# Sixteen partitions of the last load through GpSimd's software queue, in an RMSNorm-Swish kernel

## The chip, the cores and the metric

The kernel runs on one core of one Trainium2 chip. The metric is the device time of one execution in microseconds (us), as the median of several executions. An execution's time is about 1.3 us longer than the span of its profile (161.31 us and 160.0 us).

## The reference

```python
x = randn(16, 1024, 512); gamma = ones(512); eps = 1e-5      # float32
rms = sqrt(mean(x ** 2, axis=-1, keepdims=True) + eps)
x_norm = x / rms * gamma
out = x_norm * sigmoid(x_norm)
```

The kernel reads 33.6 MB and writes 33.6 MB.

## The kernel before

The 16384 rows are cut into eleven tiles. A tile is [128 partitions, sz rows each, 512], so a partition's piece of a tile of 8 rows is 16 KB, contiguous in memory. SyncE issues all loads, ScalarE issues all stores, each on a hardware queue of its own. The tiles lie in a ring of 96 row slots; tile 10, the last one, takes the slots of the second half of tile 3 and so can be loaded once store 3 has landed.

```python
sizes = [4, 4, 8] + [16] * 6 + [8, 8]
ring = 96; cn = 4                         # a chunk is 4 row slots
...
def load(t):
    ...                                   # waits for the stores whose slots it takes
    return nc.sync.dma_start(out=buf(t), in_=dram(xf, t)).then_inc(ld[t], 16)
...
for k in range(K):                        # GpSimd: (mean square + eps) ** -0.5, 32 chunks
    need(nc.gpsimd.tensor_scalar(out=aeps[:, k, :], in0=ms[:, k, :], ...), s_sum, k + 1)...
    need(nc.gpsimd.tensor_tensor(out=rstd[:, k, :], ..., op=ALU.pow), s_eps, k + 1)...
...
def store(t):                             # ScalarE
    need(nc.scalar.dma_start(out=dram(of, t), in_=buf(t)), s_swish, ends[t]).then_inc(st[t], 16)
```

ScalarE squares (3 rows into PSUM, 1 row with its own accumulator), VectorE sums the squares and multiplies by the row's factor and gamma, ScalarE applies Silu in place.

## Time and profile before

| | before |
|---|---|
| time, median of 3 | 160.29 us (160.28 to 160.62) |
| the profiled execution | 161.31 us, span 160.0 us |
| busy | VectorE 87%, ScalarE 78%, GpSimd 41% |
| DMA | 420 GB/s on average, 67.14 MB |

The page of the kernel before: the DMA rows of the slices (40 slices of 4 us; busy tenths, then GB/s), the queues (q1 is SyncE's, q10 ScalarE's; packets, MB, share of the 16 engines' time), and the chain that ended last.

```profile
DMA  6999999989999999999999999999999999999994
GB/s 250 444 487 393 393 381 455 475 358 477 426 408 442 414 483 395 418 483 410 401 461 451 393 442 459 401 451 442 426 393 455 414 442 442 467 401 405 430 434 180
...
q1 hardware_dynamic: 1584, 33.56, 49.3%
q10 hardware_dynamic: 1592, 33.56, 48.8%
q14 instruction: 3, 0.02, 0.0%
...
DVE xb L215 48%; DVE ms L204 29%; DMA xb<-in_x_dram 13%; ACT xb L178 1%; ACT sq L166 1%; ACT junk L159 0%; SPq L118 0%; ACTq L158 0%
```

The chain names VectorE, and VectorE indeed never pauses between 25 and 148.8 us. But the two queues together hold the 16 DMA engines for 98% of the span. To decide between the two, look at the end. This is the timeline of the kernel before (start, duration, engine, line, operation; in brackets the idle time before):

```profile
143.81 0.34 ACTq L183 DMA_DIRECT2D out_dram<-xb  x1
144.33 1.39 POOL L148 TENSOR_TENSOR rstd<-aeps,neg_half 128x4 f32<-128x4 f32 x1
146.18 1.91 ACT L178 ACTIVATE xb<-xb 128x2048 f32<-128x2048 f32 x1 [2.40 <-DVE xb L215]
148.83 1.91 ACT L178 ACTIVATE xb<-xb 128x2048 f32<-128x2048 f32 x1 [0.74 <-DVE xb L215]
150.77 0.34 ACTq L183 DMA_DIRECT2D out_dram<-xb  x1
```

The last two stores (2 MB each) are issued at 143.81 and 150.77 us. In these transfers each of the sixteen DMA engines increments the transfer's semaphore (a counter that other engines wait on) when its share has landed, so the trace has sixteen landings of each:

```
store 9 :  153.06 153.13 153.14 153.25 153.26 153.30 153.37 153.42 153.43 153.44 153.47 153.53 153.71 153.72 153.90 155.11
store 10:  157.91 157.98 157.99 158.09 158.12 158.16 158.21 158.26 158.28 158.29 158.31 158.37 158.55 158.56 158.74 159.96
```

When store 10 is issued, store 9 still needs 2.3 us. Store 10 then lands one transfer time (eight packets of 16 KB that follow each other every 0.607 us, 4.86 us) after store 9. The end is thus bound by the DMA engines; VectorE has some 2 us of slack (an estimate from these 2.3 us). One engine is 1.2 us late.

### The profile page before, as it was taken

The page shows a single profiled execution, that of the slowest core. Times are in us where ns is not written, and L with a number is a line of the kernel's source. Part 1 is how long each engine was busy: PE and PEld are TensorE (multiplying, and loading weights), DVE is VectorE, ACT ScalarE, POOL GpSimd, SP SyncE. Part 2 cuts the span into 40 slices and gives each one's busy share as a digit, 9 for nine tenths or more (in the row PEclk, how much of TensorE's full clock was granted, in tenths as well). Part 3 has the DMA queues.
Part 4 walks back from the last instruction along what each step waited for, and adds up shares of the span by engine and source line. Part 5 has one row for each costly group of instructions (what it writes and reads, how often), then busy time and mean ns, then how long its engine had stood idle before and what let it go on. Part 6 is the DMA issues. An engine that isn't in the chain of part 4 may idle for free.

```text
span 160.0 us, 437 instructions
## 1 busy us (share of the span) xinstructions
DVE 139.1 (87%) x162; ACT 125.1 (78%) x129; POOL 65.5 (41%) x70
## 2 busy tenths in 40 slices
DVE  0298986999999999999999999999999999999100
ACT  1839849888888889988888888888899888884400
POOL 1043552444555555444444445555554444444000
DMA  6999999989999999999999999999999999999994
GB/s 250 444 487 393 393 381 455 475 358 477 426 408 442 414 483 395 418 483 410 401 461 451 393 442 459 401 451 442 426 393 455 414 442 442 467 401 405 430 434 180
DMA packets 3179, 67.14 MB, mean 420 GB/s; under 512 B 356, under 2 KB 356, under 8 KB 360
## 3 DMA queue, kind: packets, MB, share of 16 engines
q1 hardware_dynamic: 1584, 33.56, 49.3%
q10 hardware_dynamic: 1592, 33.56, 48.8%
q14 instruction: 3, 0.02, 0.0%
HBM read 33.56 MB, written 33.55 MB: 419 GB/s over the span
## 4 chain that ended last, share of the span: by engine, by line
DVE 77%; DMA 13%; ACT 2%; issue 0%; SPq 0%; ACTq 0%
DVE xb L215 48%; DVE ms L204 29%; DMA xb<-in_x_dram 13%; ACT xb L178 1%; ACT sq L166 1%; ACT junk L159 0%; SPq L118 0%; ACTq L158 0%
## 5 line engine op out<-in xcount | busy, mean ns | idle before, releaser
L215 DVE SCALAR_TENSOR_TENSOR xb<-xb,rstd,gamma_sb 128x512 f32<-128x512 f32 x128 | 87.4, 747 | 0.0
L178 ACT ACTIVATE xb<-xb 128x2048 f32<-128x2048 f32 x32 | 61.1, 1908 | 16.3 <-DVE xb L215 16.3
L204 DVE TENSOR_REDUCE ms<-sq 128x3 f32<-128x1536 f32 x32 | 56.1, 1754 | 9.7 <-ACT sq L166 9.6
L141 POOL TENSOR_SCALAR aeps<-ms 128x4 f32<-128x4 f32 x32 | 20.7, 646 | 75.9 <-DVE ms L204 75.9
L166 ACT ACTIVATE sq<-xb 128x1536 f32<-128x1536 f32 x32 | 45.9, 1433 | 0.0
L148 POOL TENSOR_TENSOR rstd<-aeps,neg_half 128x4 f32<-128x4 f32 x32 | 44.0, 1376 | 2.7
L159 ACT ACTIVATE junk<-xb 128x512 bf16<-128x512 f32 x32 | 19.7, 615 | 5.7 <-DMA xb<-in_x_dram 5.7
L159 ACT ACTIVATION_READ_ACCUMULATOR junk<-xb 128x1 f32 x32 | 6.0, 187 | 0.0
L190 ACT ACT_TABLE_LOAD x1 | 1.3, 1283 | 3.6 <-issue 3.6
L136 POOL MEMSET gamma<- 128x512 f32 x1 | 0.5, 526 | 1.5 <-POOLq L65 1.5
L228 DVE STREAM_SHUFFLE gamma_sb<-gamma 128x512 f32<-128x512 f32 x1 | 0.7, 720 | 0.0
L255 POOL MEMSET const-float32-0.0<- 128x1 f32 x1 | 0.1, 99 | 0.2 <-issue 0.2
L255 POOL MEMSET const-bfloat16-1.0<- 128x1 bf16 x1 | 0.1, 103 | 0.0
L255 POOL MEMSET const-uint8-127<- 128x1 uint8 x1 | 0.1, 102 | 0.0
L137 POOL MEMSET neg_half<- 128x4 f32 x1 | 0.1, 102 | 0.0
L255 POOL MEMSET const-float32-1.0<- 128x1 f32 x1 | 0.1, 99 | 0.0
L228 DVE LOAD_MASK_SELECT gamma_sb<-gamma x1 | 0.0, 15 | 0.0
## 6 DMA issues: line engine op xcount, KB each, us to landing
xb<-in_x_dram SPq DMA_DIRECT2D x6, 4096.0 KB, 44.5
out_dram<-xb ACTq DMA_DIRECT2D x6, 4096.0 KB, 29.8
xb<-in_x_dram SPq DMA_DIRECT2D x3, 2048.0 KB, 38.5
out_dram<-xb ACTq DMA_DIRECT2D x3, 2048.0 KB, 11.3
xb<-in_x_dram SPq DMA_DIRECT2D x2, 1024.0 KB, 5.9
out_dram<-xb ACTq DMA_DIRECT2D x2, 1024.0 KB, 19.8
gamma<-in_gamma_dram ACTq DMA_DIRECT2D x1, 8.0 KB
```

The costliest lines, as they stand in the source:

```text
L136: nc.gpsimd.memset(gamma4, 0.0).then_inc(s_zero, 1)
L137: nc.gpsimd.memset(neg_half, -0.5).then_inc(s_half, 1)
L141: nc.gpsimd.tensor_scalar(out=aeps[:, k, :], in0=ms[:, k, :], scalar1=eps_f, scalar2=None, op0=ALU.add,),
L148: nc.gpsimd.tensor_tensor(out=rstd[:, k, :], in0=aeps[:, k, :], in1=neg_half, op=ALU.pow),
L159: acc = nc.scalar.activation(out=junk[k % 2], in_=xb[:, at + n_sq, :], func=AF.Square, scale=inv_d**0.5, accum_out=ms[:, k, n_sq : n_sq + 1],)
L166: square = nc.scalar.activation(out=sq[k % 2][:, 0:n_sq, :], in_=xb[:, at : at + n_sq, :], func=AF.Square, scale=inv_d**0.5,)
L178: nc.scalar.activation(out=rows, in_=rows, func=AF.Silu), s_norm, k + 1
L190: nc.scalar.preload_act_table_set("silu_and_others")
L204: nc.vector.tensor_reduce(out=ms[:, k, 0:n_sq], in_=sq[k % 2][:, 0:n_sq, :], op=ALU.add, axis=mybir.AxisListType.X,),
L215: ins = nc.vector.scalar_tensor_tensor(out=row, in0=row, scalar=rstd[:, k, j : j + 1], in1=gamma_sb, op0=ALU.mult, op1=ALU.mult,)
L228: nc.vector.stream_shuffle(gamma_sb, gamma4, [0] * 32), s_gld, 16
L255: nc = _bacc.Bacc("TRN2", target_bir_lowering=False, num_devices=1)
```

## The change

The intent is to even out the DMA engines: engines 0 to 3 are held to be the late ones (the trace does not number the engines). Sixteen of the 128 partitions of the last load, one eighth of it, leave SyncE's queue and go through GpSimd's, first twelve, then four. Tiny transfers of 4 and 8 rows between them are to turn that queue's choice of engines, so that the twelve fall on engines 4 to 15 and the four on 4 to 7. The core of the diff:

```diff
+    blank = [sbuf(f"blank{i}", [8, 16]) for i in range(3)]
...
+    split = 112
     def load(t):
...
+        if t == T - 1:
+            return nc.sync.dma_start(
+                out=buf(t)[0:split], in_=dram(xf, t)[0:split]
+            ).then_inc(ld[t], 16)
         return nc.sync.dma_start(out=buf(t), in_=dram(xf, t)).then_inc(ld[t], 16)
...
+    def turn(count):
+        nc.gpsimd.dma_start(
+            out=blank.pop()[0:count, :], in_=gamma[0 : 16 * count].rearrange("(p n) -> p n", n=16)
+        ).then_inc(s_turn[0], 16)
+        s_turn.pop(0)
+
+    def load_rest(t):
+        ...                               # waits for store 3
+        nc.gpsimd.dma_start(
+            out=buf(t)[split : split + 12], in_=dram(xf, t)[split : split + 12]
+        ).then_inc(s_rest[0], 16)
+        turn(4)
+        nc.gpsimd.dma_start(
+            out=buf(t)[split + 12 : P], in_=dram(xf, t)[split + 12 : P]
+        ).then_inc(s_rest[1], 16)
+        turn(8)
+
+    turn(4)
     for k in range(K):
+        if k == 19:
+            load_rest(T - 1)
...                                       # ScalarE, before the first chunk of tile 10:
+            if t == T - 1:
+                nc.scalar.wait_ge(s_rest[0], 16)
+                nc.scalar.wait_ge(s_rest[1], 16)
```

More of the change, by code (lines that the diff above doesn't have):

```diff
@@ L81 @@
     st = [nc.alloc_semaphore(f"st{t}") for t in range(T)]
+    blank = [sbuf(f"blank{i}", [8, 16]) for i in range(3)]
+    s_turn = [nc.alloc_semaphore(f"s_turn{i}") for i in range(3)]
+    s_turns = list(s_turn)
+    s_rest = [nc.alloc_semaphore(f"s_rest{i}") for i in range(2)]
     s_gld = nc.alloc_semaphore("s_gld")
@@ L138 @@
     nc.gpsimd.wait_ge(s_half, 1)
+    def turn(count):
[4 more added lines that the diff above has]
+    def load_rest(t):
+        _, sz, at = tiles[t]
+        for u in range(t):
+            if tiles[u][2] < at + sz and at < tiles[u][2] + tiles[u][1]:
+                nc.gpsimd.wait_ge(st[u], 16)
+        nc.gpsimd.dma_start(
[7 more added lines that the diff above has]
+    turn(4)
     for k in range(K):
+        if k == 19:
+            load_rest(T - 1)
         need(
@@ L233 @@
             norm(k - 1)
+    for sem in s_turns:
+        nc.sync.wait_ge(sem, 16)
     for t in range(T):
```

## The prediction

> **What bounds the kernel now.** The chain of waits ends on VectorE (77%), and VectorE has no gap from 25 us to 148.8 us. I nevertheless read the end as bound by the DMA engines. The last store (2 MB) is issued at 150.77 us and lands at 159.96 us. The landings of the last four stores (one increment of the semaphore per DMA engine, read from the trace) follow each other by just the time of their packets: 138.5-139.2, 148.2-149.0, 153.1-153.9, 157.9-158.7 us. So at 150.77 the engines still hold 2.3 us or more of the store before; VectorE has that much slack. The page's slices show DMA at 9 tenths or more almost everywhere, 420 GB/s on average.
>
> In each of these stores one engine of the sixteen lands late: 140.57, 150.26, 155.11, and 159.96 against 158.74 for the next. Followed back packet by packet, this engine moved as many bytes as the others but lost some 1.2 us in stalls after 45 us (a 0.3 us gap at 48.0, longer packets near 81, 101, 121 and 127 us). A 16 KB packet takes 0.611 us, so it is two packets late, and it alone sets the end.
>
> **What the change does.** Load 10 (2 MB, landed 133.3 us) shrinks from 8 to 7 packets of 16 KB per engine. Sixteen partitions go through GpSimd: 12 meant for engines 4-15, then 4 meant for engines 4-7[...]. Engines 0-3 then carry one packet less, 8-15 as before, 4-7 one more. [...]
>
> **Worth on the critical path.** If the late engine is one of 0-3 (the gamma load of 4 rows marks four engines, two with the same 0.3 us gap; the late one isn't marked, but my tracing is uncertain in the first 20 us), its end moves by -0.61 us; engines 4-7 move by +0.61, from at most 158.4 to 159.0 (last packets). Best case: about 159.7 us. If it is another engine: 0 to +0.6 us.
>
> **Costs.**
> - GpSimd issues four transfers before chunk 19 (about 89 us; their buffer is free, store 3 landed at 79.6). GpSimd idles some 2.2 us per chunk of 4.3 us. [...]
> - [...]
>
> **Prediction.** 160.0 us, range 159.2 to 161.6. Faster by over 2%: 1%; within 2%: 93%; slower by over 2%: 6%.
>
> **What would show it.** Right: the straggler of the last store lands about 0.6 us after the others, not 1.2; four engines have 99 packets' worth of bytes less one; VectorE's gap near 90 us is under 2.3 us; the last store still queues behind the one before. Wrong: the straggler keeps 1.2 us (not among 0-3, or the sixteen partitions fell on other engines); packets of load 10 longer than 0.611 us [...]; VectorE idle over 2.3 us near chunk 19, with the DMA running dry before the last store.
>
> **What would make it wrong.** [...] stalls of a DMA engine that wander from run to run, so that no fixed choice of engines helps.

The forecast came to 160.0 us, range 159.2 to 161.6: the 160.29 us known of the kernel before, 0.61 us less at best or up to 0.6 us more if the late engine is another, and two costs on top, for the time of GpSimd's issues and for the writes to the sixteen partitions.

## The result and the profile after

The time went from 160.28 us (median of 4, 160.17 to 160.62) to 164.56 us (median of 4, 164.28 to 165.68). The ratio is 1.0276, with a 95% interval of 1.0226 to 1.0326: slower. Ratios here are the mean time of one kernel's fast runs over that of the other's fast runs of the same rounds, so they are not quite the ratio of the medians quoted. The profile after is of an execution of 164.28 us.

The page of the kernel after, the same lines as before. q0 is GpSimd's software queue.

```profile
DMA  6998998998999999999999999999999999999992
GB/s 249 448 462 386 402 485 356 430 501 360 438 404 422 466 436 434 402 491 402 418 475 394 426 298 380 438 406 414 446 458 410 414 446 426 426 450 394 426 438 117
...
q1 hardware_dynamic: 1568, 33.29, 49.2%
q10 hardware_dynamic: 1592, 33.56, 48.1%
q0 software_dynamic: 160, 0.26, 0.6%
q14 instruction: 3, 0.02, 0.0%
...
DVE xb L252 47%; DVE ms L241 29%; DMA xb<-in_x_dram 13%; ACT xb L215 1%; ACT sq L203 1%; ACT junk L196 0%; SPq L128 0%; ACTq L192 0%
```

The chain of waits looks as before and explains nothing: VectorE still never pauses. The difference is in the GB/s row: slices 24 and 25 (94 to 102 us) fell from 442 and 459 to 298 and 380. The engines are still counted as fully busy there (9 tenths): they hold packets, but the packets take longer.

The same in four stretches of the kernel before and then of the kernel after (stretch in us, its length, busy time of VectorE, ScalarE and GpSimd with instruction counts, clock, DMA share, GB/s):

```profile
85.00:92.00 7.00, 7.00 (x9) 6.09 (x7) 2.55 (x4) 1.00 1.00 431
92.00:100.00 8.00, 8.00 (x10) 7.09 (x9) 3.91 (x4) 1.00 1.04 451
100.00:108.00 8.00, 8.00 (x11) 7.09 (x9) 4.09 (x4) 1.00 0.99 426
108.00:116.00 8.00, 8.00 (x11) 7.10 (x9) 4.09 (x4) 1.00 1.01 434
```

```profile
85.00:92.00 7.00, 7.00 (x8) 6.09 (x7) 4.65 (x8) 1.00 1.03 445
92.00:100.00 8.00, 8.00 (x10) 7.09 (x8) 3.73 (x4) 1.00 1.01 337
100.00:108.00 8.00, 8.00 (x11) 7.09 (x9) 4.09 (x4) 1.00 1.00 418
108.00:116.00 8.00, 8.00 (x11) 7.09 (x9) 4.09 (x4) 1.00 1.00 430
```

VectorE and ScalarE are as busy as before in every stretch. From 92 to 100 us the DMA moved 337 in place of 451 GB/s at the same share of busy time.

This is what GpSimd spends on it, from the timeline of the kernel after:

```profile
89.41 0.61 POOL L161 DMA_DIRECT2D xb<-in_x_dram  x1
89.79 1.75 DVE L241 TENSOR_REDUCE ms<-sq 128x3 f32<-128x1536 f32 x1
89.91 1.91 ACT L215 ACTIVATE xb<-xb 128x2048 f32<-128x2048 f32 x1 [0.46 <-DVE xb L252]
90.01 0.52 POOL L151 DMA_DIRECT2D blank<-in_gamma_dram  x1
90.52 0.52 POOL L165 DMA_DIRECT2D xb<-in_x_dram  x1
91.03 0.52 POOL L151 DMA_DIRECT2D blank<-in_gamma_dram  x1
91.46 2.73 DVE L252 SCALAR_TENSOR_TENSOR xb<-xb,rstd,gamma_sb 128x512 f32<-128x512 f32 x4
91.64 0.65 POOL L175 TENSOR_SCALAR aeps<-ms 128x4 f32<-128x4 f32 x1
```

Four issues take 2.1 us and just fit into the idle time that GpSimd has in a chunk (2.2 us). Nobody waits for them. The last store is issued at 150.64 us, no later than before (150.77), and lands 3 us later:

```
store 10 after:  159.62 159.80 159.81 160.04 160.12 160.16 160.33 160.36 160.40 160.44 160.49 160.93 161.37 162.11 162.71 162.93
```

Two things have happened to the landings. All engines are later: the mean of the sixteen went from 158.36 to 160.72 us. And they have drawn apart: four of them stand 0.4 to 2 us behind the twelfth.

The packets show the first of these directly. An undisturbed packet of 16 KB takes 0.611 us and one of 32 KB takes 1.213 us; after 50 us, nine in ten packets of the kernel after keep to that within 3 ns. I call the time above that a packet's excess, and sum it over all packets from 50 us on; beside the sum I count the packets with more than 0.1 us. Before, the excess is 1.7 us, with 4 such packets. After, it is 35.6 us, with 53, and 33.0 us of it falls between 88 and 116 us, while the sixteen partitions are moved: seven of the sixteen packets took 1.0 to 1.3 us instead of 0.611, and 32 KB packets of SyncE's queue at that time took up to 1.99 us longer. 35.6 us over sixteen engines are 2.2 us each.

### The profile page after: what moved, and what is told of

Read it like the earlier page. It is cut to its first block, busy times and chain, and to the rows that moved or that the text cites. A ratio compares the mean times of both kernels' runs of the same rounds, so it can differ in the third digit from the quotient of the medians.

```text
span 163.0 us, 443 instructions
## 1 busy us (share of the span) xinstructions
DVE 139.1 (85%) x162; ACT 125.2 (77%) x129; POOL 68.3 (42%) x75
## 4 chain that ended last, share of the span: by engine, by line
DVE 76%; DMA 13%; ACT 2%; issue 0%; SPq 0%; ACTq 0%
DVE xb L252 47%; DVE ms L241 29%; DMA xb<-in_x_dram 13%; ACT xb L215 1%; ACT sq L203 1%; ACT junk L196 0%; SPq L128 0%; ACTq L192 0%
## 5 line engine op out<-in xcount | busy, mean ns | idle before, releaser
L151 POOL DMA_DIRECT2D blank<-in_gamma_dram x3 | 1.8, 590 | 0.3 <-POOL neg_half L147 0.3
L161 POOL DMA_DIRECT2D xb<-in_x_dram x1 | 0.6, 609 | 0.0
L165 POOL DMA_DIRECT2D xb<-in_x_dram x1 | 0.5, 518 | 0.0
```

The source lines that it names most:

```text
L151: nc.gpsimd.dma_start(out=blank.pop()[0:count, :], in_=gamma[0 : 16 * count].rearrange("(p n) -> p n", n=16)).then_inc(s_turn[0], 16)
L161: nc.gpsimd.dma_start(out=buf(t)[split : split + 12], in_=dram(xf, t)[split : split + 12]).then_inc(s_rest[0], 16)
```

## The experiments

Three theories, and a fourth question:

- **Partitions** (the expectations call it the port theory). Packets that are written at the same time to these sixteen partitions, 112 to 127, hold each other up. The runs can show whether the partitions written make the difference.
- **Software queue.** GpSimd's queue itself, or its extra packets (128 of its 160 are of 4 bytes), slows the engines.
- **Placement.** The packets fell on other engines than intended, and the uneven counts are the loss.
- And: was the late engine of the profile before a property of the kernel at all?

Each experiment was correct against the reference. The first four ran together on one chip, and so did the next four. Kernel before beside them: 160.28 us (160.04 to 160.60). The diffs are shortened; those of the first five runs are against the kernel after.

### The same partitions from a hardware queue

```diff
-        nc.gpsimd.dma_start(out=buf(t)[112:124], ...)     # and [124:128], with three turns
+        nc.scalar.wait_ge(st[3], 16)
+        nc.scalar.dma_start(out=buf(t)[112:124], ...)     # and [124:128], no turns
```

> The same 12 and 4 partitions are loaded from ScalarE's hardware queue at the same chunk; GpSimd issues no transfer and nothing turns. Port theory [...]: the loss stays, 163 to 165 us, with packets lengthened by 0.3 to 2 us while these 16 packets move, in sum 20 to 35 us. Software-queue theory (GpSimd's queue itself costs the DMA engines their time): back to 160 to 161 us, no lengthened packets. Placement alone [...]: 160.9 us, one packet of 0.61 us later than before.

Measured: 163.85 us (163.82 to 165.22), ratio 1.0245 (1.0203 to 1.0288). Excess: 36.0 us, 53 packets over 0.1 us. The slow stretch moved with the transfers, which now stand in line behind ScalarE's stores and landed at 117 to 121 us. The same four stretches of this run:

```profile
85.00:92.00 7.00, 7.00 (x9) 6.09 (x7) 2.55 (x4) 1.00 1.00 431
92.00:100.00 8.00, 8.00 (x10) 7.09 (x8) 3.90 (x4) 1.00 1.04 451
100.00:108.00 8.00, 8.00 (x11) 7.09 (x9) 4.09 (x4) 1.00 0.97 418
108.00:116.00 8.00, 8.00 (x11) 7.09 (x9) 4.67 (x3) 1.00 1.04 346
```

No GpSimd transfer is left, and nearly the whole loss is. On this queue the loads of twelve and of four partitions have twelve and four landings (and one update each at their issue), so twelve engines and four take part. Followed from packet to packet (the way is described under the tiny transfers below), the four are the engines of the gamma load, have one of the twelve packets as well, and land last, the last of them 2.0 us behind the mean.

The last store was issued later in this run, at 152.10 us. ScalarE's two extra issues (85.8 and 86.2 us) are not the reason. From 113.4 us on GpSimd's addition of eps took 2.65 us in place of 0.66, and at the end VectorE waited for GpSimd once (who waited for whom: us in total, times, longest us):

```profile
DVE xb L239 <- POOL rstd L155: 1.2, 1, 1.2
```

Why GpSimd slowed there is not known. The store before the last landed from 153.90 to 157.68 us, so the DMA engines were not idle at 152.10 us and the delay did not set the end.

### The same bytes from GpSimd, as a row of every partition

```diff
-            out=buf(t)[0:112], in_=dram(xf, t)[0:112]                  # SyncE
+            out=buf(t)[:, 0:7, :], in_=dram(xf, t)[:, 0:7, :]
-            out=buf(t)[112:124] ...                                    # GpSimd, two and three turns
+            out=buf(t)[:, 7:8, :], in_=dram(xf, t)[:, 7:8, :]          # GpSimd, one transfer
```

> GpSimd's queue moves the same 256 KB of the last load, but as one row of all 128 partitions instead of sixteen whole partitions[...]. Port theory: 160 to 161 us, few lengthened packets near 93 us. Software-queue theory: 162.5 us or more, as after the change.

Measured: 160.52 us (160.39 to 160.54), ratio 1.0015 (1.0000 to 1.0030). Excess: 1.2 us. The slow stretch of this run, and then its software queue:

```profile
92.00:100.00 8.00, 8.00 (x10) 7.09 (x8) 3.77 (x4) 1.00 0.99 425
```

```profile
q0 software_dynamic: 80, 0.26, 0.4%
```

The same 0.26 MB through the same software queue cost nothing that matters. The software-queue theory falls. (The packets are of another size here, 64 of 4 KB in place of 16 of 16 KB. The pair of runs with sixteen neighbouring and with every eighth partition, below, leaves the size alone.)

### The tiny transfers alone

```diff
-            out=buf(t)[0:112] ...                         # SyncE
+            out=buf(t) ...                                # whole again
-        nc.gpsimd.dma_start(out=buf(t)[112:124] ...)      # and [124:128]
         turn(4)                                           # the three turns stay
         turn(8)
```

> Only the three tiny transfers through GpSimd; the last load is whole again on the hardware queue. Port and placement theories: 160.0 to 160.8 us. Software-queue theory (cost by the transfer, not by the byte): 161.5 us or more. [...]

Measured: 160.28 us (160.17 to 160.40), ratio 1.0002 (0.9986 to 1.0017). They are free. They also did not do what they were for, which was to turn the queue's choice of engines. The trace does not number the engines, so I followed each engine from packet to packet: the next packet of an engine starts within a few ns of the end of the last, and each engine is given eight packets and one semaphore write of every transfer of 128 partitions on the hardware queues, as the counts of the kernel before have it (its eleven loads have sixteen landings each and left 1584 packets, 11 × 16 × 9). Two engines can be taken for one another where they are in step, so this is a reconstruction, not a record. Four engines hold the gamma load of 4 rows. The first turn of 4 rows lies on the same four. The second turn of 4 lies on three of these and a fourth that I take for the other one, swapped on the way; the turn of 8 holds three of them, that one, and four others. Resolved another way, the ties put the second turn on two engines of the gamma load and two others. In both, the turn of 8 holds all four engines of the turn before it, where a queue that moves on would have left them out.

### One transfer of sixteen partitions, no turns

```diff
-        nc.gpsimd.dma_start(out=buf(t)[112:124] ...)      # turn(4), [124:128], turn(8)
+        nc.gpsimd.dma_start(out=buf(t)[112:128], in_=dram(xf, t)[112:128])
-    turn(4)
```

> One GpSimd transfer of all sixteen partitions, no tiny transfers: one packet for each engine, so all engines carry equal bytes again. Port theory: still slow, 162.5 to 165 us, with lengthened packets in sum 20 to 35 us. Placement theory (the engines' uneven counts are the loss): back to 160.0 to 160.6 us. Software-queue theory: between, since there is one transfer in place of five.

Measured: 162.62 us (161.81 to 162.89), ratio 1.0140 (1.0103 to 1.0178). Excess: 35.1 us, as after the change. The software queue left 32 packets, as many as a data packet and a semaphore write for each of sixteen engines. But the landings of the last store lie close together again (the last at 161.09 us, 0.6 us above the mean of 160.46; after the change the last stands 2.2 us above its mean). So the loss has two parts of about the same size: 2.3 us because packets take longer, and 1.9 us more when the sixteen go as twelve and four.

### The change without its turns

```diff
-    turn(4)              # before the loop; and turn(4), turn(8) inside load_rest
```

> The change without its three tiny transfers: GpSimd issues the transfers of 12 and of 4 partitions, nothing between. If the queue hands out engines in a circle, 12 and then 4 fill all sixteen engines evenly, and the time falls to that of one transfer of 16, 162.6 us. If every transfer starts at engine 0 (so the tiny ones turned nothing), the four lowest engines still get two packets each, the time stays at 164.0 to 165.0 us, and four landings of the last store stand 1 to 2.5 us behind the rest.

Measured: 164.30 us (163.22 to 165.02), ratio 1.0257 (1.0199 to 1.0315). The last four landings are 161.34, 161.51, 162.06 and 162.38 us, against a mean of 160.47. Twelve and then four, dealt in a circle, would fill sixteen engines evenly and give the 162.6 us of the run before. They do not: the time stays that of the full change. The reconstruction agrees: four engines have both, eight have one, four have none, and the four with both are the four that land last. In that of the full change, too, four engines have both; they are the last three and the fifth from the end, and at least three of them are engines of the gamma load.

### Sixteen neighbouring partitions against every eighth

These two kernels are the kernel before plus four GpSimd loads of 128 KB into a spare buffer, sixteen partitions of 8 KB each, at chunks 12, 16, 20 and 24. They differ only in the partitions written.

```diff
+            nc.gpsimd.dma_start(out=spare[112:128], in_=dram(xf, T - 1)[112:128, 0:4, :])   # first kernel
+            nc.gpsimd.dma_start(out=spare[0:128:8], in_=dram(xf, T - 1)[112:128, 0:4, :])   # second kernel
```

> The kernel before, with four extra GpSimd loads of 128 KB into a spare buffer, on partitions 112 to 127. The bytes alone cost 4 times 0.3 us, so 161.5 us. Port theory: [...] 163.5 to 165.5 us, with lengthened packets in sum 35 to 60 us.

> As the run before it with the same bytes, packets and queue, but on every eighth partition[...]. Port theory: [...] 161.8 to 163 us, with lengthened packets in sum 10 to 20 us, a third of the other's. If sixteen-partition transfers are slow as such, both are equally slow.

| | time (us) | ratio, 95% | profiled execution | excess | mean landing of the last store |
|---|---|---|---|---|---|
| partitions 112 to 127 | 164.48 (163.92 to 164.61) | 1.0257 (1.0234 to 1.0281) | 164.61 us | 52.6 us, 91 packets over 0.1 us | 162.81 us |
| every eighth partition | 162.95 (162.16 to 163.31) | 1.0162 (1.0128 to 1.0195) | 162.16 us | 7.7 us, 28 packets over 0.1 us | 160.02 us |

The GB/s row of the page of the first and then of the second; both moved 67.67 MB:

```profile
GB/s 265 435 458 433 341 506 363 419 502 387 411 427 421 458 456 413 405 385 474 443 311 474 393 458 251 466 401 421 421 373 445 482 417 425 409 482 393 405 441 301
```

```profile
GB/s 244 450 481 391 391 418 416 471 367 467 471 414 399 424 454 399 456 464 399 432 424 448 424 432 424 397 448 440 401 430 444 436 428 456 424 424 448 391 440 261
```

The first dips to 311 and to 251 where two of its four transfers run (slices 21 and 25), the second nowhere. Source, bytes, packets and queue are the same and the intervals of the ratios do not overlap, so the partitions written make the difference; by what mechanism is not shown.

How large it is, is less certain. In the profiles the second's excess is a seventh of the first's, not the third that I expected. But the first profile is of the slowest of its four executions and the second of the fastest. By the medians the two are 4.20 and 2.67 us over the kernel before; less 1.22 us for the bytes that is 3.0 and 1.5 us, about a half. So every eighth partition may not be free either.

Within each profile the excess accounts for the mean landing. An engine's packets of 8 KB follow each other every 0.306 us, so four times 128 KB are 4 × 0.306 = 1.22 us for each engine. Take the excess over that of the kernel before (1.1 us in its second profile, below) and spread it on 16 engines. Then the first should be late by 1.22 + (52.6 − 1.1) / 16 = 4.4 us and is late by 162.81 − 158.34 = 4.5 us; the second by 1.22 + (7.7 − 1.1) / 16 = 1.6 us and is late by 1.7 us.

### The kernel before, profiled again

> The kernel before once more, for a second profile. If the late engine of the first profile (1.2 us behind in the last store, in an execution that took 161.3 us, 1 us over the median) is a property of the kernel, it is late by 1.2 us again; if it was that execution's, the last landing stands 0.3 to 0.7 us behind the next and the span is 159.0 us.

Measured: one execution of 160.06 us (state unknown), span 158.7 us. Landings of the last store: 157.88 to 158.59 us, and the last at 158.70 us. No engine is late. The queues of that run hold 98.8% of the engines' time:

```profile
q1 hardware_dynamic: 1584, 33.56, 49.7%
q10 hardware_dynamic: 1592, 33.56, 49.1%
```

In this execution, then, the lateness was absent: it belonged to the one that was first profiled, which at 161.31 us was 1 us over the kernel's median. What delayed it there is not known; one packet of 32 KB took 0.56 us longer at 126.9 us, with nothing else to be seen beside it.

## Why the prediction was wrong

The time predicted was 160.0 us (159.2 to 161.6); it was 164.56 us. Point by point:

- **The DMA engines bound the end, not VectorE.** Right. VectorE's work was not touched in the change, and the time follows the landings in every run.
- **The cost of writing to the sixteen partitions.** This is the step that failed. The prediction allowed a small cost for it, for a reason that no trace had shown. Measured: 35.6 us of excess in place of 1.7, which is 2.1 us for each engine, 2.3 us of time in the run with one transfer of sixteen. The longer packets of the sixteen themselves, seven of 1.0 to 1.3 us instead of 0.611, are not all of it. By the reconstruction of the full change even the four engines that carried none of the sixteen lost 1.9 to 2.3 us between 93 and 103.5 us, each mostly in one 32 KB packet of SyncE's queue of 3.0 to 3.1 us. What these four waited for was not tested. The 32 KB packet that took 1.99 us longer came, by the reconstruction, right behind one of the sixteen on its engine; whether it waited because of that was not tested either.
- **"12 meant for engines 4-15, then 4 meant for engines 4-7."** The prediction priced mainly the case that the queue's choice of engines turns. This is the second step that failed: it does not for these transfers. In the trace of the kernel after, each of the five GpSimd transfers, of 4, 8 and 12 partitions, has sixteen landings, where the gamma load of 4 rows on ScalarE's hardware queue has four (and one update at its issue). The five left 160 packets, 32 for each: 16 of 16 KB, 16 of 64 bytes and 128 of 4 bytes. That is as many as a data packet, or a 4-byte one in its place, and a semaphore write for each of sixteen engines in each transfer. So, by the reconstruction, four engines got both packets, three of them at least engines of the gamma load: 7 + 2 against 7 + 1 and 7 + 0. Going as twelve and four cost another 1.9 us. The four packets of the second group took only 0.61 to 0.91 us, so their own lengthening is not the bulk of it. By the reconstruction the engine that lands last has one packet more than the mean (0.61 us) and 3.2 us of excess against a mean of 2.2; together 1.6 of the 1.9 us. Why its packets waited longer than the others' is not shown.
- **"It alone sets the end"**, the engine 1.2 us late. The reading was right for that execution and wrong for the kernel. In the second profile (state unknown) the last engine is 0.36 us behind the mean landing (158.70 and 158.34 us), so even a perfect rebalancing had only that to win there, not 0.61 us.
- **The time of GpSimd's issues.** The prediction's figure for it, and the delay of VectorE that followed from it, rested on no trace. Measured: 0.52 to 0.61 us per issue in the loop, and VectorE was held back by nothing.

The sum for the change, from the profiles: the mean landing moved from 158.34 us (second profile of the kernel before) to 160.72 us, +2.4 us, and the distance from the mean to the last grew from 0.36 to 2.21 us, +1.85 us. Together 4.2 us; the spans differ by 163.0 − 158.7 = 4.3 us.

What stays open: what sixteen partitions cost when they are every eighth one (the time, 162.95 us, lay inside the 161.8 to 163 us expected, the excess of the one profile, 7.7 us, under the 10 to 20 us); whether GpSimd's queue turns for other kinds of transfers (stores were not tried); and how much of the loss comes from the 112 partitions of the main load, whose stretch (116 to 136 us) holds 2.3 of the 35.6 us of excess, and 6.0 of 35.1 us in the run with one transfer of sixteen. No kernel that beats the kernel before came out of this: the software-queue version by rows and the tiny transfers alone both only equal it.

## What to carry to other kernels

Before splitting a transfer by partitions, check which partitions the packets will be written to: the sixteen neighbouring partitions 112 to 127 cost 1.4 to 2.8% here although they were an eighth of one load, while the same bytes as a row of every partition cost nothing. A DMA share of 100% can hide a lost quarter of the bandwidth (337 for 451 GB/s), so read the GB/s row and the packets' durations beside it. And before balancing against a late engine, profile a second execution and see whether it is late again.
